# Two rings of weight buffers and sixteen activation buffers, spread over the address modulo 512

## The chip, the cores and the metric

The kernel is one program on one core of a Trainium2 chip. A core has a matrix engine (PE), a vector engine (DVE), a scalar engine (ACT), a general engine (POOL) and a queue engine (SP) that issues most DMAs here. Each engine works through its own list of instructions in order, and engines wait for each other by semaphores. SBUF is the on-chip memory of 128 partitions, PSUM the memory that PE writes its products to. The metric is the time of one execution on the device, in microseconds (us).

## The reference, cut to what matters

Two transformer blocks over 1024 tokens of width 1024, all in float32: the first has two layers (a window attention mixer and a linear recurrence mixer, each with attention to a memory, and an MLP of width 4096), the second has one layer of stick-breaking and sliding-window attention. Nearly all of the arithmetic is in products with weights:

```python
x = x + jnp.concatenate([mixed, mo], axis=-1) @ w_out[l]
x = x + squared_relu_mlp(rms_norm(x, mlp_norm[l]), w_up[l], w_down[l])
def squared_relu_mlp(h, w_up, w_down):
    return jnp.square(jax.nn.relu(h @ w_up)) @ w_down
```

## The kernel before, in words

Activations lie transposed: 128 features on the partitions, 1024 tokens along them, in two halves of 512. A float32 operand is split into two numbers of the matrix engine's type, `hi` and `lo` (`split`: ACT casts to `hi`, DVE subtracts to get `lo`), and a product is three matmuls, hi·hi, lo·hi and hi·lo (`mm3`, L121, L124, L125). Each is a weight load of 128x128 and a matmul of up to 512 columns.

`weight` fetches 128x1024 raw weights by a DMA on SP's queue into a tile `wr`, and splits them into tiles `wh` and `wl`. These two names are rings of four buffers each in the pool `wp`. The activations of the matmuls lie in eight tiles `hh0` to `hh7` and eight `hl0` to `hl7` in the pool `hp` (`h_tiles`; named `uh`, `ul`, `oph`, `opl` where other stages use the same buffers), and in stages that need more in further tiles `xh`, `xl` of the pool `hx`.

The first layer's stages are memory keys, attention, the output projection (`down_groups`), the MLP's up phase and its down phase; the second layer's and the second block's follow in the same manner. The up phase computes 16 units of weights, each by seven half-size products (Strassen's scheme, `up_phase`), out of operands `B11`, `B21`, `T1` to `T4` and `B22` that `first_ops` and `other_ops` make from the normalised activations with DVE, ACT and POOL. `early_products` does what needs `B11` and `B21` alone for the first five units while the others are made. Of one unit, the weights come as two raw tiles; DVE forms sums in `v` (L749 to L751) and in place in the raw tiles, then the pair `yh`, `yl` (for `A11` and `S3`), the pair `xh`, `xl` (for `A22` and `A12`), `vh`, `vl` (for `S1`, `S2`) and `qh`, `ql` (for `S4`) are split. Of the first five units, `A22` is the first half of the second raw tile, which no sum changes before. The y and x pairs come from the same rings `wh` and `wl`.

The order of the instructions on each engine is made when the program is built: a scheduler takes the instructions by priority and by its own model of time, and gives a tile a buffer of its tag when one is free. So a different set of tags can give a different order, though the source's order is the same.

Of the kernel before, what the change touches and what calls it, by code (L numbers as in the profile page):

```python
# [11 lines left out]
F32 = mybir.dt.float32  # L12
F32R = mybir.dt.float32r
# [8 lines left out]
P = 128  # L22
D = 1024
S = 1024
KC = D // P
# [21 lines left out]
def net_kernel(ctx: ExitStack, tc: tile.TileContext, xT, memT, vecs, pos, sinks, invf, mask0, alibi,  # L47
# [5 lines left out]
    wp = ctx.enter_context(tc.tile_pool(name="wp", bufs=1))  # L53
    dp = ctx.enter_context(tc.tile_pool(name="dp", bufs=1, space=DRAM))
    hp = ctx.enter_context(tc.tile_pool(name="hp", bufs=1, side="right"))
# [26 lines left out]
    def nm(base):  # L82
        n_name[0] += 1
        return f"{base}_{n_name[0]}"
# [14 lines left out]
    def split(hi, lo, src, hi_eng=None, lo_eng=dve):  # L99
        if hi_eng is dve:  # L100
            dve.tensor_copy(hi, src)
        else:
            act.copy(hi, src)  # L103
        lo_eng.tensor_tensor(out=lo, in0=src, in1=hi.bitcast(F32), op=ALU.subtract)  # L104
# [5 lines left out]
    def weight(src, n=1024, hi_eng=None, lo_eng=dve):  # L110
        raw = wp.tile([P, 1024], F32, tag="wr", name=nm("wr"), bufs=4)
        nc.sync.dma_start(raw[:, :n], src)
        hi = wp.tile([P, 1024], F32R, tag="wh", name=nm("wh"), bufs=4)
        lo = wp.tile([P, 1024], F32R, tag="wl", name=nm("wl"), bufs=4)
        split(hi[:, :n], lo[:, :n], raw[:, :n], hi_eng, lo_eng)
        return hi, lo

# [86 lines left out]
    def spread(r, n, tmp, psp):  # L204
        dg = tmp.tile([P, 512], F32, tag="sq", name=nm("dg"))
        for j in range(n // P):
            dve.tensor_scalar(out=dg[:, j * P:j * P + P], in0=ident, scalar1=r[:, j:j + 1], scalar2=None, op0=ALU.mult)
        pr = psp.tile([P, 512], F32, tag="po", name=nm("psr"))
        pe.matmul(pr[:, :n], ones, dg[:, :n], start=True, stop=True)
        return pr  # L210

    def norm_r(sums, tmp, psp, rtile, first=False, rtile2=None, keep=None):
# [17 lines left out]
            dve.tensor_copy(keep, r)  # L230
        act.copy(rtile, spread(r, n, tmp, psp)[:, :n])

    def h_tiles():
        hh = [hp.tile([P, S], F32R, tag=f"hh{c}", name=nm("hh")) for c in range(KC)]
        hl = [hp.tile([P, S], F32R, tag=f"hl{c}", name=nm("hl")) for c in range(KC)]
        return hh, hl
# [37 lines left out]
    def down_groups(x, order, load_u, pieces, up, psp, sums, after_half, cuts=(hs(0), hs(1)), halves=False):  # L274
        for gi, gs_ in enumerate(order):
# [4 lines left out]
            def fetch(q, gs_=gs_):  # L280
                ws[q] = [weight(pieces[g * 4 + q]) for g in gs_]
# [160 lines left out]
    hh, hl = h_tiles()  # L442
    with tc.tile_pool(name="s0", bufs=1) as tp, \
# [19 lines left out]
        for l in range(2):  # L463
            mkh = tp.tile([P, 4, ML], F32R, tag="mkh", name=nm("mkh"))
            mkl = tp.tile([P, 4, ML], F32R, tag="mkl", name=nm("mkl"))
            for h in range(4):
                wh, wl = weight(w_memk[l * 4 + h]) if l + h else w00
# [11 lines left out]
            for q in range(4):  # L479
                wh, wl = weight(w_memv[l * 4 + q])  # L480
# [225 lines left out]
    def prod(ps, w, op, start=True):  # L706
        hi, lo, o = w
        mm3(ps, [(hi[:, o + k * P:o + k * P + P], lo[:, o + k * P:o + k * P + P], op[0][k], op[1][k])
                 for k in range(4)], start=start, skip=True)

    def square_out(l, cc, src, f, th):
        act.activation(cc, src, AF.Relu)
        act.activation(cc, cc, AF.Square)
        nc.sync.dma_start(u_d[l][:, f, hs(th)], cc)

    def raw_half(src, parts):
        raw = wp.tile([P, 1024], F32, tag="wr", name=nm("wr"), bufs=4)
        for i, o in enumerate(parts):
            n = 1024 // len(parts)
            nc.sync.dma_start(raw[:, i * n:i * n + n], src[:, o:o + n])  # L720
        return raw

    def early_products(l, ops, tk):
        banks = {}
        for i in range(EARLY + 1):
            if i < EARLY:
                raw = raw_half(w_up[l * 16 + i], (0, 1536))
                hi = wp.tile([P, 1024], F32R, tag="wh", name=nm("wh"), bufs=4)
                lo = wp.tile([P, 1024], F32R, tag="wl", name=nm("wl"), bufs=4)
                split(hi, lo, raw)  # L730
                ps = psp.tile([P, HT], F32, "S", nm("psu"))
                prod(ps, (hi, lo, 0), ops["B11"])
                e1 = tk.tile([P, HT], F32, tag="ru", name=nm("e1"))
                act.copy(e1, ps)
                nc.sync.dma_start(e_d[l][:, i, :], e1)
                banks[i] = (ps, hi, lo)
            if i:
                ps, hi, lo = banks[i - 1]
                prod(ps, (hi, lo, 512), ops["B21"], start=False)
                cc = tk.tile([P, HT], F32, tag="ru", name=nm("cc"))  # L740
                square_out(l, cc, ps, 2 * i - 2, 0)

    def up_phase(l, ops, up):
        def weights(i, part):
            r1 = raw_half(w_up[l * 16 + i], (0,))
            r2 = raw_half(w_up[l * 16 + i], (1024,))
            a11, a21, a22, a12 = r1[:, :512], r1[:, 512:], r2[:, :512], r2[:, 512:]
            v = up.tile([P, 1024], F32, tag="v", name=nm("v"), bufs=1)
            dve.tensor_tensor(out=v[:, :512], in0=a21, in1=a22, op=ALU.add)  # L749
            dve.tensor_tensor(out=a21, in0=a11, in1=a21, op=ALU.subtract)  # L750
            dve.tensor_tensor(out=v[:, 512:], in0=v[:, :512], in1=a11, op=ALU.subtract)  # L751

            def pair():
                return (wp.tile([P, 1024], F32R, tag="wh", name=nm("wh"), bufs=4),
                        wp.tile([P, 1024], F32R, tag="wl", name=nm("wl"), bufs=4))

            (yh, yl), (xh, xl) = pair(), pair()
            y0, x1 = (512, 512) if part else (0, 1024)
            split(yh[:, y0:], yl[:, y0:], r1[:, y0:])
            split(xh[:, :x1], xl[:, :x1], r2[:, :x1])  # L760
            vh = up.tile([P, 1024], F32R, tag="vh", name=nm("vh"), bufs=2)
            vl = up.tile([P, 1024], F32R, tag="vl", name=nm("vl"), bufs=2)
            split(vh, vl, v)
            dve.tensor_tensor(out=a12, in0=a12, in1=v[:, 512:], op=ALU.subtract)
            qh = up.tile([P, 512], F32R, tag="qh", name=nm("qh"), bufs=2)
            ql = up.tile([P, 512], F32R, tag="ql", name=nm("ql"), bufs=2)
            split(qh, ql, a12)
            return {"A11": (yh, yl, 0), "S3": (yh, yl, 512), "A22": (xh, xl, 0), "A12": (xh, xl, 512),
                    "S1": (vh, vl, 0), "S2": (vh, vl, 512), "S4": (qh, ql, 0)}

        def small(tag, bufs):
            return up.tile([P, HT], F32, tag=tag, name=nm(tag), bufs=bufs)

        tail = None
        for i in range(16):
            part = i < EARLY
            w = weights(i, part)
            a = psp.tile([P, HT], F32, "mm", nm("psu"))
            e1 = small("e", 4)
            if part:  # L780
                nc.sync.dma_start(e1, e_d[l][:, i, :])
            else:
                prod(a, w["A11"], ops["B11"])
                act.copy(e1, a)
                b = psp.tile([P, HT], F32, "tr", nm("psu"))
                prod(b, w["A12"], ops["B21"])
                cc = small("cc", 4)
                dve.tensor_tensor(out=cc, in0=e1, in1=b, op=ALU.add)
                square_out(l, cc, cc, 2 * i, 0)
            if tail:  # L790
                tail()
            c = psp.tile([P, HT], F32, "S", nm("psu"))
            prod(c, w["S1"], ops["T1"])

            def add_to(a, e1, part=part):
                t = small("e", 4)
                if part:
                    dve.tensor_tensor(out=t, in0=e1, in1=a, op=ALU.add)
                else:
                    act.copy(t, a)  # L800
                return t

            prod(a, w["S2"], ops["T2"], start=part)
            u1 = add_to(a, e1)
            d = psp.tile([P, HT], F32, "tr", nm("psu"))
            prod(d, w["A22"], ops["T4"])
            prod(a, w["S3"], ops["T3"], start=False)
            u2 = add_to(a, e1)
            cc = small("cc", 4)
            dve.tensor_tensor(out=cc, in0=u2, in1=c, op=ALU.add)  # L810
            square_out(l, cc, cc, 2 * i + 1, 1)
            cc = small("cc", 4)
            dve.tensor_tensor(out=cc, in0=u2, in1=d, op=ALU.subtract)
            square_out(l, cc, cc, 2 * i + 1, 0)

            def tail(i=i, w=w, c=c, u1=u1):
                prod(c, w["S4"], ops["B22"], start=False)
                cc = small("cc", 4)
                dve.tensor_tensor(out=cc, in0=u1, in1=c, op=ALU.add)
                square_out(l, cc, cc, 2 * i, 1)  # L820
        tail()
# [34 lines left out]
    for l in range(2):  # L856
# [169 lines left out]
        with ExitStack() as ph:  # L1026
# [81 lines left out]
            hh, hl = nh[-1]  # L1108
# [349 lines left out]
```

## Time and profile before

| | us |
|---|---|
| three runs | 3061.18, 3063.29, 3067.44 |
| median | 3063.29 |
| the profiled execution | 3062.59 |
| its span, from the first to the last instruction | 3060.8 |

In the profile "PE" is matmuls and "PEld" weight loads, which overlap them. A matmul's duration runs to its modelled end, so consecutive matmuls overlap in the records, and what counts is the distance from start to start. "Idle before" is the time in which an engine did nothing before an instruction, with the instruction that ended it. "PEclk" is the granted clock of TensorE as a share of its upper level of 2.4 GHz; 0.50 is the lower level of 1.2 GHz.

### The profile page before, as it was taken

What the parts mean: (1) busy time and instruction counts of PE and PEld (TensorE: products, weight loads), DVE (VectorE), ACT (ScalarE), POOL (GpSimd) and SP (SyncE); (2) the same over time, 40 slices, a digit from 0 to 9 for tenths busy, and PEclk for the clock granted to TensorE, in tenths of its full rate; (3) what the DMA queues carried; (4) which work ended last, traced back from release to release, by engine and by line L of the source; (5) the groups of instructions that cost most, each with busy time, mean ns of one, the idle gap of its engine ahead of it and who ended that gap; (6) DMA issues with size and microseconds to landing.
All of it is one profiled execution on the core that took longest, in us unless ns stands there. A gap on an engine that the chain in (4) does not pass through costs nothing. (4 is left out here: it accounts for less than half of the span.)

```text
span 3060.8 us, 38811 instructions
## 1 busy us (share of the span) xinstructions
PE 2936.4 (96%) x14624; PEld 2395.3 (78%) x14624; DVE 1793.7 (59%) x3053; ACT 1308.9 (43%) x2408; POOL 395.1 (13%) x428
## 2 busy tenths in 40 slices
PE   8999999989999999998889979999999999999998
PEld 7988778768888888776767858888888777777777
DVE  7666754674457443678874575445343565666555
ACT  6566541444552121356772344554121244444542
POOL 3222100300000000333320210000000211111112
PEclk9999999989999999999999989999999999999999
DMA  7111244343357322221246234237232121111152
GB/s 263 42 49 63 95 169 175 119 148 110 104 175 258 131 97 90 69 66 66 88 159 235 101 107 139 103 125 237 76 104 76 55 76 42 35 42 56 64 178 77
DMA packets 136204, 341.55 MB, mean 112 GB/s; under 512 B 14928, under 2 KB 29520, under 8 KB 136016
## 3 DMA queue, kind: packets, MB, share of 16 engines
q1 hardware_dynamic: 131840, 331.93, 31.7%
q10 hardware_dynamic: 4176, 7.13, 0.7%
q8 instruction: 115, 1.88, 0.3%
q14 instruction: 73, 0.60, 0.1%
HBM read 245.16 MB, written 93.85 MB: 111 GB/s over the span
## 5 line engine op out<-in xcount | busy, mean ns | idle before, releaser
L124 PE MATMUL psd<-ul,wh 128*128 128x512 f32 (+1 forms) x1568 | 606.9, 387 | 1.2 <-DMA ul<-mixl 1.2
L121 PE MATMUL psd<-uh,wh 128*128 128x512 f32 (+1 forms) x1568 | 606.5, 387 | 0.9 <-DVE x L315 0.8
L125 PE MATMUL psd<-uh,wl 128*128 128x512 f32 (+1 forms) x1568 | 606.0, 387 | 0.0
L103 ACT CAST wh<-wr 128x1024 fp32r<-128x1024 f32 (+2 forms) x236 | 234.6, 998 | 729.5 <-PE psd L124 497.0
L104 DVE TENSOR_TENSOR wl<-wr,wh 128x1024 fp32r<-128x1024 f32 (+2 forms) x260 | 311.1, 1199 | 220.9 <-ACT wh L103 219.7
L315 DVE TENSOR_TENSOR x<-x,psd 128x512 f32<-128x512 f32 x288 | 196.5, 685 | 377.4 <-PE psd L125 371.3
L121 PEld LDWEIGHTS psd<-uh,wh 128*128 128x128 f32 x1568 | 294.7, 188 | 61.9 <-issue 2.0
L124 PEld LDWEIGHTS psd<-ul,wh 128*128 128x128 f32 x1568 | 294.7, 188 | 61.3 <-issue 2.1
L125 PEld LDWEIGHTS psd<-uh,wl 128*128 128x128 f32 x1568 | 294.8, 188 | 60.1 <-issue 1.9
L121 PE MATMUL psu<-oph,wh 128*128 128x512 f32 x512 | 200.7, 394 | 41.2 <-ACT wh L103 41.2
L153 POOL TENSOR_TENSOR acc<-acc,sq 128x512 f32<-128x512 f32 (+1 forms) x70 | 94.6, 1352 | 1006.7 <-ACT sq L149 995.6
L124 PE MATMUL psu<-opl,wh 128*128 128x512 f32 x512 | 199.9, 391 | 0.0
L125 PE MATMUL psu<-oph,wl 128*128 128x512 f32 x512 | 199.0, 391 | 0.0
L124 PE MATMUL pj<-hl,wh 128*128 128x512 f32 x416 | 165.1, 401 | 9.1 <-DVE hl L104 9.1
L121 PE MATMUL pj<-hh,wh 128*128 128x512 f32 x416 | 169.3, 411 | 4.3 <-DVE qkl L104 2.2
L125 PE MATMUL pj<-hh,wl 128*128 128x512 f32 x416 | 164.9, 400 | 0.0
L121 PEld LDWEIGHTS psu<-oph,wh 128*128 128x128 f32 x512 | 96.8, 189 | 62.4 <-ACT wh L103 42.1
L124 PEld LDWEIGHTS psu<-opl,wh 128*128 128x128 f32 x512 | 96.7, 189 | 20.4 <-issue 0.5
L125 PEld LDWEIGHTS psu<-oph,wl 128*128 128x128 f32 x512 | 96.6, 189 | 20.2
L121 PE MATMUL psx<-hh,wh 128*128 128x512 f32 x256 | 98.5, 396 | 6.9 <-ACT gl L896 6.9
L121 PE MATMUL psu<-oph,vh 128*128 128x512 f32 x256 | 100.8, 394 | 0.0
L124 PE MATMUL psu<-opl,vh 128*128 128x512 f32 x256 | 100.6, 393 | 0.0
(335 smaller groups left out, 5916.8 us busy)
## 6 DMA issues: line engine op xcount, KB each, us to landing
wr<-in_w_up SPq DMA_DIRECT2D x64, 512.0 KB, 3.9
ud<-cc SPq DMA_DIRECT2D x128, 256.0 KB, 2.2
ur<-ud SPq DMA_DIRECT2D x64, 512.0 KB, 3.6
wr<-in_w_down SPq DMA_DIRECT2D x64, 512.0 KB, 4.0
wr<-in_w_out SPq DMA_DIRECT2D x32, 512.0 KB, 3.6
wr<-in_w_in SPq DMA_DIRECT2D x26, 512.0 KB, 3.5
wra<-in_w_ada SPq DMA_DIRECT2D x24, 512.0 KB, 4.4
uh<-mixh SPq DMA_DIRECT2D x20, 512.0 KB, 8.1
```

The lines of the kernel that those rows point to most:

```text
L103: act.copy(hi, src)
L104: lo_eng.tensor_tensor(out=lo, in0=src, in1=hi.bitcast(F32), op=ALU.subtract)
L121: ins = pe.matmul(out, lh, rh, start=start and i == 0, stop=False, skip_group_check=skip)
L124: pe.matmul(out, lh, rl, start=False, stop=False, skip_group_check=skip)
L125: ins = pe.matmul(out, ll, rh, start=False, stop=stop and i == n - 1, skip_group_check=skip)
L153: pool.tensor_tensor(out=self.acc[:, :n], in0=self.acc[:, :n], in1=sq[:, :n], op=ALU.add)
L315: dve.tensor_tensor(out=xs, in0=xs, in1=ps, op=ALU.add)
```

## The change

The rings `wh` and `wl` become four tags of one buffer each, taken in turn (`ring`), and behind each of these eight buffers lies an unused tile of 16 float32 (64 bytes a partition). Behind each of the sixteen activation buffers lies an unused tile of 8 float32 (32 bytes), set when `h_tiles` is called first. No instruction is added or taken away: the lists of the five engines have the same lengths, and only the order differs.

```diff
-        hi = wp.tile([P, 1024], F32R, tag="wh", name=nm("wh"), bufs=4)
-        lo = wp.tile([P, 1024], F32R, tag="wl", name=nm("wl"), bufs=4)
+        hi = ring("wh")
+        lo = ring("wl")
...
+    pads, used, pads_done = [], {}, []
+
+    def pad(pool_, width):
+        pads.append(pool_.tile([P, width], F32, tag=f"pad{len(pads)}", name=f"pad{len(pads)}"))
+
+    def ring(name):
+        i = used.setdefault(name, 0)
+        used[name] = i + 1
+        t = wp.tile([P, 1024], F32R, tag=f"{name}{i % 4}", name=nm(name))
+        if i < 4:
+            pad(wp, 16)
+        return t
+
     def h_tiles():
+        if not pads_done:
+            pads_done.append(True)
+            hh, hl = [], []
+            for out, t in ((hh, "hh"), (hl, "hl")):
+                for c in range(KC):
+                    out.append(hp.tile([P, S], F32R, tag=f"{t}{c}", name=nm(t)))
+                    pad(hp, 8)
+            return hh, hl
```

`early_products` and the y and x pairs of `up_phase` call `ring` in the same way. The byte addresses within a partition, modulo 512, in the two built programs:

| buffers | before | now |
|---|---|---|
| `wh`, four | 480, each | 480, 96, 224, 352 |
| `wl`, four | 480, each | 32, 160, 288, 416 |
| `hh`, eight | 480, each | 480, 0, 32, 64, 96, 128, 160, 192 |
| `hl`, eight | 480, each | 224, 256, 288, 320, 352, 384, 416, 448 |
| tiles of `hx`, of `x`, of `vh`, `vl`, `qh`, `ql` | 480, each | 480, each |

Of the 11,968 matmuls with split operands, the moving and the stationary operand stood 0 bytes apart modulo 512 in 11,776 before; the other 192, of the memory attention, stood 128 (96) and 384 (96) apart. Now 2,026 stand 0 apart, and each of the other multiples of 32 has 430 to 1,144.

The order differs in the up phase of both layers and in a few places behind them. The first place is where the up phase of the first layer begins. On PE, before: `psu_1329` is the last early product, `wh_1338` the weights of `A22` of unit 0, `oph_1295` and `opl_1297` the first two blocks of `T4`, `vh_1340` the weights of `S1` and `S2`.

```order
L125 MATMUL psu_1329_6501<-oph_1255_6071,wl_1328_6498 128x512
L121 MATMUL psu_1348_6610<-oph_1295_6282,wh_1338_6565 128x512
L124 MATMUL psu_1348_6610<-opl_1297_6284,wh_1338_6565 128x512
L121 MATMUL psu_1346_6583<-oph_1279_6266,vh_1340_6571 128x512
L124 MATMUL psu_1346_6583<-opl_1281_6268,vh_1340_6571 128x512
L121 MATMUL psu_1344_6580<-oph_1287_6274,vh_1340_6571 128x512
L124 MATMUL psu_1344_6580<-opl_1289_6276,vh_1340_6571 128x512
```

On PE now, at the same place; `wh_1357` are the weights of `A22` of unit 1.

```order
L125 MATMUL psu_1329_6525<-oph_1255_6095,wl_1328_6522 128x512
L121 MATMUL psu_1348_6634<-oph_1295_6306,wh_1338_6589 128x512
L121 MATMUL psu_1368_6743<-oph_1295_6306,wh_1357_6681 128x512
L124 MATMUL psu_1348_6634<-opl_1297_6308,wh_1338_6589 128x512
L125 MATMUL psu_1348_6634<-oph_1295_6306,wl_1339_6590 128x512
L121 MATMUL psu_1348_6634<-oph_1295_6306,wh_1338_6589 128x512
L124 MATMUL psu_1368_6743<-opl_1297_6308,wh_1357_6681 128x512
```

All 24 matmuls of the two products with `T4` now stand ahead of the first one with `vh_1340`; two stood there before. The same holds at the start of the second layer's up phase.

On DVE, before, behind the last of the operands: the sums of unit 0 (`v_1335`, and `wr` in place) and the low parts of its weights.

```order
L749 TENSOR_TENSOR v_1335_6559<-wr_1333_6555,wr_1334_6557 128x512
L750 TENSOR_TENSOR wr_1333_6555<-wr_1333_6555 128x512
L751 TENSOR_TENSOR v_1335_6559<-v_1335_6559,wr_1333_6555 128x512
L764 TENSOR_TENSOR wr_1334_6557<-wr_1334_6557,v_1335_6559 128x512
L104 TENSOR_TENSOR wl_1337_6564<-wr_1333_6555,wh_1336_6563 128x512
L104 TENSOR_TENSOR wl_1339_6566<-wr_1334_6557,wh_1338_6565 128x512
L104 TENSOR_TENSOR vl_1341_6572<-v_1335_6559,vh_1340_6571 128x1024
```

On DVE now, some 26 instructions earlier, among the operands:

```order
L104 TENSOR_TENSOR opl_1286_6297<-x_1135_5338,oph_1284_6295 128x512
L104 TENSOR_TENSOR wl_1339_6590<-wr_1334_6581,wh_1338_6589 128x512
L717 TENSOR_TENSOR x_1132_5335<-x_1132_5335 128x512
...
L724 TENSOR_TENSOR x_862_4129<-t2_1299_6317,x_862_4129 128x512
L104 TENSOR_TENSOR opl_1289_6300<-t2_1299_6317,oph_1287_6298 128x512
L104 TENSOR_TENSOR wl_1358_6682<-wr_1353_6673,wh_1357_6681 128x512
```

Two low parts, `wl_1339` and `wl_1358`, have moved ahead of most of the operands, and so have their casts `wh_1338` and `wh_1357` on ACT. The sums of unit 0 still stand behind all operands.

## Rows read from the trace of the kernel before

**Rows 1.** The page: the span, PE's busy time, and PE and its granted clock in 40 slices of the span.

```profile
span 3060.8 us, 38811 instructions
PE 2936.4 (96%) x14624; PEld 2395.3 (78%) x14624; DVE 1793.7 (59%) x3053; ACT 1308.9 (43%) x2408; POOL 395.1 (13%) x428
PE   8999999989999999998889979999999999999998
PEclk9999999989999999999999989999999999999999
```

**Rows 2.** Who PE waited for in the whole span: us in total, times, longest.

```profile
PE psu L121 <- ACT wh L103: 41.2, 2, 21.6
...
PE pj L124 <- DVE hl L104: 9.1, 2, 7.2
...
PE ms L121 <- ACT mp L380: 7.2, 2, 6.8
...
PE psr L209 <- DVE dg L207: 3.8, 2, 3.5
PE pj L121 <- DVE qkl L104: 2.2, 2, 1.9
PE pj L121 <- ACT hh L103: 2.2, 1, 2.2
```

**Rows 3.** Busy time of each engine in stretches around the start of the up phase, in both layers, with the count of instructions: start and end, length, PE, PEld, DVE, ACT, POOL, then the granted clock, DMA share and GB/s.

```profile
606.00:626.00 20.00, 0.44 (x2) 0.01 (x1) 17.99 (x26) 8.58 (x16) 10.03 (x4) 0.58 0.28 92
626.00:629.70 3.70, 3.67 (x8) 2.65 (x9) 3.68 (x6) 1.45 (x2) 0.00 (x0) 0.50 0.40 138
629.70:640.00 10.30, 10.30 (x47) 8.51 (x46) 10.15 (x15) 4.21 (x6) 0.00 (x0) 1.00 0.59 187
640.00:850.00 210.00, 210.00 (x928) 173.98 (x927) 110.82 (x148) 102.73 (x159) 0.00 (x0) 1.00 0.35 119
...
1781.20:1802.90 21.70, 0.09 (x1) 0.00 (x0) 19.69 (x29) 9.42 (x18) 10.97 (x4) 0.55 0.10 34
```

**Rows 4.** PE in order of time at the start of both up phases: start, us, engine, line, operation, tiles. In the first layer, the last early product's last matmul, then the first, second, third, tenth and 25th matmul behind the wait; in the second layer the first.

```profile
606.05 0.39 PE L125 MATMUL psu<-oph,wl 128*128 128x512 f32 x1
626.03 0.79 PE L121 MATMUL psu<-oph,wh 128*128 128x512 f32 x1 [19.60 <-ACT wh L103]
626.63 0.63 PE L124 MATMUL psu<-opl,wh 128*128 128x512 f32 x1
627.05 0.72 PE L121 MATMUL psu<-oph,vh 128*128 128x512 f32 x1
...
629.98 0.39 PE L125 MATMUL psu<-oph,wl 128*128 128x512 f32 x1
...
633.40 0.39 PE L124 MATMUL psu<-opl,vh 128*128 128x512 f32 x1
```

```profile
1802.92 0.79 PE L121 MATMUL psu<-oph,wh 128*128 128x512 f32 x1 [21.63 <-ACT wh L103]
```

**Rows 5.** DVE in order of time in the first of these stretches.

```profile
609.71 0.68 DVE L104 TENSOR_TENSOR opl<-t,oph 128x512 fp32r<-128x512 f32 x1
612.20 1.92 DVE L104 TENSOR_TENSOR opl<-x,oph 128x512 fp32r<-128x512 f32 x2 [1.80 <-ACT oph L103]
...
621.00 2.48 DVE L104 TENSOR_TENSOR opl<-x,oph 128x512 fp32r<-128x512 f32 x4
623.41 0.68 DVE L749 TENSOR_TENSOR v<-wr,wr 128x512 f32<-128x512 f32 x1
624.12 0.69 DVE L750 TENSOR_TENSOR wr<-wr 128x512 f32<-128x512 f32 x1
624.73 0.69 DVE L751 TENSOR_TENSOR v<-v,wr 128x512 f32<-128x512 f32 x1
```

**Rows 6.** ACT in order of time in the same stretch.

```profile
611.55 0.62 ACT L103 CAST oph<-x 128x512 fp32r<-128x512 f32 x1 [3.97 <-POOL x L701]
...
624.84 1.14 ACT L103 CAST wh<-wr 128x512 fp32r<-128x512 f32 x2 [3.72 <-DVE wr L750]
625.89 1.04 ACT L103 CAST vh<-v 128x1024 fp32r<-128x1024 f32 x1
```

**Rows 7.** POOL's subtraction that makes `T4`: all eight of the span (shortest, median and longest in ns), and its place in order of time.

```profile
L701 POOL TENSOR_TENSOR x<-t,x x8: 1264/1645/6459, 605.1 to 1794.0; 128x512 f32<-128x512 f32 x8
```

```profile
605.06 7.69 POOL L701 TENSOR_TENSOR x<-t,x 128x512 f32<-128x512 f32 x2 [22.87 <-DVE t L699]
```

**Rows 8.** PE in order of time: matmuls of 256 columns back to back, first with operands 384 bytes apart modulo 512, then 128, then 0; of each the first and the last of seven.

```profile
343.24 0.29 PE L124 MATMUL ms<-mkl,mqh 128*128 128x256 f32 x1
...
343.96 0.29 PE L125 MATMUL ms<-mkh,mql 128*128 128x256 f32 x1
```

```profile
1577.97 0.28 PE L124 MATMUL ms<-mkl,mqh 128*128 128x256 f32 x1
...
1578.69 0.28 PE L124 MATMUL ms<-mkl,mqh 128*128 128x256 f32 x1
```

```profile
3019.13 0.28 PE L124 MATMUL psd<-ul,wh 128*128 128x256 f32 x1
...
3019.85 0.28 PE L124 MATMUL psd<-ul,wh 128*128 128x256 f32 x1
```

**Rows 9.** The weight loads of the down products, as a group over the span: busy us, mean ns of one.

```profile
L124 PEld LDWEIGHTS psd<-ul,wh 128*128 128x128 f32 x1568 | 294.7, 188 | 61.3 <-issue 2.1 <-DMA ul<-mixl 1.6
```

More of the change, by code (lines that the diff above doesn't have):

```diff
@@ L727, in early_products @@
                 raw = raw_half(w_up[l * 16 + i], (0, 1536))
-                hi = wp.tile([P, 1024], F32R, tag="wh", name=nm("wh"), bufs=4)
-                lo = wp.tile([P, 1024], F32R, tag="wl", name=nm("wl"), bufs=4)
+                hi = ring("wh")
+                lo = ring("wl")
                 split(hi, lo, raw)
@@ L753, in pair @@
             def pair():
-                return (wp.tile([P, 1024], F32R, tag="wh", name=nm("wh"), bufs=4),
-                        wp.tile([P, 1024], F32R, tag="wl", name=nm("wl"), bufs=4))
+                return (ring("wh"),
+                        ring("wl"))
             (yh, yl), (xh, xl) = pair(), pair()
```

## The prediction

> **What bounds the kernel now.** I read the page first. It shows PE busy for 2936.4 of 3060.8 us, with the clock at its upper level in nearly every slice [rows 1]. So the time is the number of PE's matmuls by their spacing, plus some 124 us in which PE does nothing. A change can win or lose in two ways: in the spacing, or in PE's waits.
>
> Then the views that answer for the spacing. In the steady stretch from 640 to 850 us PE starts 928 matmuls of 512 columns in 210.0 us [rows 3], 226.3 ns each. Three short runs of 256-column matmuls have their operands 384, 128 and 0 bytes apart modulo 512; in each, six intervals take 0.72 us, so 120 ns [rows 8]. By the two widths a column costs (226.3 − 120) / 256 = 0.415 ns, and a matmul has a fixed part of 120 − 256 × 0.415 = 13.7 ns. The reader is to see that the three distances give one number.
>
> Last the list of PE's waits. The largest is 41.2 us in two waits for the cast `wh` on ACT [rows 2]. In order of time they are the starts of the two up phases, 19.60 and 21.63 us [rows 4]. In the first, DVE works 17.99 of 20 us, ACT 8.58 and POOL 10.03 [rows 3]: DVE and POOL make the operands `T1` to `T4`, and only then DVE forms the sums of unit 0, and only behind those does ACT cast the weights that PE wants [rows 5, 6]. PE waits though `T4` (`oph` at 611.55 on ACT, `opl` at 612.20 on DVE and behind) has long been there [rows 5, 6].
>
> **The change part by part.** *Addresses.* No instruction writes a pad, so the pads cost nothing as work. 9,750 of the 11,968 split matmuls leave distance 0. The rows show three distances only, all alike to within the 0.01 us of a row over six intervals, some 2 ns. I take 0 for the other thirteen, since they lie among the three shown, and since one matmul streams 2048 bytes of its row past 512 bytes of weights: the distance between what is being read of the two changes all through a matmul. The bounds follow as rivals: distance 0 itself costs the fixed part (13.7 ns by 9,750 is a gain of 134 us), or some distances clash, by at most a whole weight load of 188 ns [rows 9].
>
> *Rings of one buffer.* A tile must now take the next tag of the ring, not the first one free. The buffer that comes late is that of a y pair, which waits for `S3`, the last of a unit, instead of `A22`'s twelve matmuls earlier: 12 × 0.226 = 2.7 us later, against the 84 matmuls, 19 us, of the unit in between. In the steady stretch DVE works 110.8 and ACT 102.7 of 210 us [rows 3], so these casts have the slack: 0. If it were gone, one such wait a unit, 2.7 us by 32 units, would be 86 us; nothing in the rows comes near it.
>
> *The order at the start of the up phases.* `wh_1338`, `wh_1357` and their low parts stand earlier, so the 24 matmuls of `A22` with `T4` can run within the wait. They need `T4` alone of the operands. First what that costs on DVE: two subtractions of 128x512, which follow each other at 0.62 us (four in 2.48 [rows 5]), 1.2 us, placed before the last operands. Before these DVE has 1.80 us idle, waiting for `oph`, and that waits 3.97 us on ACT for POOL's L701 [rows 5, 6]. Does the idle time hide the 1.2 us? POOL's two subtractions start at 605.06 and the slowest of the eight takes 6.46 us where the shortest takes 1.26 [rows 7]. From 605.06 that is an end at 611.52, which is 1.13 us after DVE went idle (609.71 + 0.68 = 610.39 [rows 5]): the subtraction looks as if it had run only once DVE stood still. I take it that it again ends 1.1 us after DVE stops, so that the 1.2 us shift POOL, ACT's `oph` and the whole chain. The Trainium skill, "SBUF — State Buffer", section "Who interferes with whom", says that a DVE instruction with two SBUF inputs and a GpSimd instruction that reads SBUF contend, and that the second to issue "fully blocks"; the 6.46 against 1.26 us agree. By that rule the 1.2 us are paid; by independent engines they vanish in DVE's 1.80 us, and the lead below is larger by 1.2 us a layer.
>
> With the shift, `v` (L751, ended 624.73 + 0.69 = 625.42 [rows 5]) is there at 626.6. ACT casts `vh` next, in 1.04 us [rows 6], with one `wh` cast fewer ahead of it; the first matmul with `vh` starts near 627.8 instead of 627.05 [rows 4].
>
> Now the gain. In the new order this matmul is the 25th from the start of the wait. Before, the 25th started at 633.40 [rows 4]. So PE is 633.4 − 627.8 = 5.6 us ahead, if its clock is then up. Before, it was not: the first eight matmuls took 626.03 to 629.71, 3.68 us at a granted clock of 0.50 (1.2 GHz), after an idle stretch of 19.6 us [rows 3, 4], where 8 × 0.226 = 1.81 us would do. Now 24 matmuls are strewn over the idle stretch, and whether the clock is up at 627.8 isn't shown by any row. With the same loss of 1.87 us the lead is 3.7 us. I take the middle, 4.65 us. The second layer has the same pieces: its wait is 21.63 us, with 19.69 of 21.70 us of DVE [rows 3, 4]. Two layers: 9.3 us, bounds 7.4 and 11.2.
>
> *What is late next.* Behind the first `vh` matmul PE runs at full spacing and DVE has 10.15 busy of 10.30 us [rows 3]: PE, being ahead, asks for `vl` and the pairs of units 1 and 2 sooner. Two low parts less in that stretch give DVE 1.2 us back there, so I count no new wait, and up to 2 us a layer if I am wrong. Further on, PE waits 9.1, 7.2, 3.8, 2.2 and 2.2 us, 24.5 us in all, for DVE and ACT in other stages [rows 2]. A lead helps in such a place only if the engine that ends the wait also gets its work sooner. Most of these waits stand behind norms, which do start from what PE made; others stand behind DVE's own queue. I take a third as given back, 3.1 us; none and three quarters are the ends. These are choices, not readings. The order also moves in the second layer's memory attention, where the 7.2 us wait is; I count it at 0, with ±2 us.
>
> **The sum.** −9.3 + 3.1 = −6.2 us on the profiled execution of 3062.59 us (span 3060.8) is 3056.4 us. That execution is 0.7 us under the median 3063.29, so 3057 us is the forecast. Its own range: nothing given back of 11.2 us, 3052 us, to three quarters of 9.3 given back, 3061 us.
>
> **The rivals.** *The lead is wholly given back.* For it: the 24.5 us of waits behind, and DVE at 10.15 of 10.30 us just after the start [rows 2, 3]. Against it: in the 210 us of steady stretch PE is full, and DVE half idle, so a lead of 5 us lives through the up phase itself. Time: 3063 us, 3060 to 3066.
>
> *Some distances clash (slower).* One place: the matmul's stream and the next weight load reading at addresses that fall on each other. A distance has (11,968 − 2,026) / 15 = 663 matmuls. If one of the 15 costs 18 ns a matmul, it takes 12 us, which beats the gain of 6 by as much again: from there it decides. At the bound, a whole load of 188 ns, it is 125 us (3182 us), at half of that 62 us (3119 us). For it: before, 11,776 matmuls stood at distance 0, so most distances have never been seen. Against it: 128 and 384 show 120 ns like 0 [rows 8]. The same section of the Trainium skill gives PE one read port for the moving operand and an independent one for weight loads, by which no distance could cost anything.
>
> *Distance 0 was the slow one.* Then the fixed part goes for 9,750 matmuls, 134 us, 2929 us, or a part of it. For it: nothing but that the fixed part's cause isn't shown. Against it: the matmuls at 384 and 128 would have to be quicker than those at 0, and are not [rows 8].
>
> **How the numbers follow.** A measurement of this kernel tells from no change about 0.2%, 6.1 us. The forecast has a chance of 0.64; since its middle lies on that bound, 0.34 of it is faster and 0.30 the same. The lead given back has 0.20, all of it the same. A clash, with any other loss of this size, has 0.12, slower. Distance 0 as the culprit has 0.04, faster. That is 0.38, 0.50 and 0.12. The range 3048 to 3068 us takes in the forecast and the lead given back with the ±2 us of the small terms in both layers; it leaves out the culprit and most of the clash, some 0.15.
>
> **What would show it.** In the profile of the changed kernel PE's two waits for `wh` must be gone or split, with matmuls of `psu` on `T4` from about 613 us, and the first with `vh` near 627.8 us; the spacing in the steady stretch must stay at 226 to 227 ns; POOL's slow subtraction must end about 1.2 us later; and what is given back must stand as longer waits for DVE in the stages behind. A spacing off by 1 ns over the 12,000 matmuls, or no lead at 640 us, would make the forecast wrong.

## The result, and the profile after

The changed kernel takes 3096.33 us (median of four runs, 3094.92 to 3100.42) where before takes 3063.38: a ratio of 1.0108, with a 95% interval of 1.0091 to 1.0126. It is 33 us slower. The forecast was 3057 us, the range ended at 3068, and "slower" had a chance of 0.12.

First the page of the changed kernel: span, PE, and PE with its granted clock in 40 slices, to be read beside [rows 1].

```profile
span 3093.1 us, 38763 instructions
PE 2981.6 (96%) x14624; PEld 2392.2 (77%) x14624; DVE 1795.9 (58%) x3053; ACT 1311.1 (42%) x2408; POOL 397.0 (13%) x428
PE   8999999999999999998889989999999989999998
PEclk9999999999999999999999989999999999999999
```

PE does as many matmuls as before, at no lower a granted clock (0.987 in the mean of the span, 0.981 before), and is busy for 45 us more. So the loss is not in waits. Then what PE waited for (us in total, times, longest), beside [rows 2]:

```profile
PE psu L121 <- ACT oph L103: 16.9, 4, 8.8
...
PE pj L124 <- DVE hl L104: 7.6, 3, 6.9
PE psu L124 <- DVE opl L104: 5.6, 2, 2.8
...
PE pj L121 <- DVE qkl L104: 3.8, 2, 3.5
...
PE psu L121 <- ACT vh L103: 1.5, 2, 1.2
```

The 41.2 us for `wh` are gone; 16.9, 5.6 and 1.5 us of waits for operands and for `vh` stand in their place. So PE waits less, as forecast, and the kernel is slower all the same. The stretches of [rows 3] show where (start and end, length, then PE, PEld, DVE, ACT and POOL busy with their counts, granted clock, DMA share, GB/s); the first three are bounded at the last early product, the first matmul with `vh`, and 640 us:

```profile
609.60:626.00 16.40, 6.48 (x16) 4.06 (x16) 14.46 (x21) 7.90 (x14) 10.52 (x4) 0.75 0.32 101
626.00:630.60 4.60, 4.45 (x10) 2.99 (x10) 4.53 (x8) 1.64 (x3) 0.00 (x0) 0.50 0.01 4
630.60:640.00 9.40, 9.32 (x39) 7.44 (x40) 8.97 (x14) 3.35 (x6) 0.00 (x0) 0.96 0.52 174
640.00:850.00 210.00, 210.00 (x908) 170.17 (x906) 114.47 (x153) 105.38 (x160) 0.00 (x0) 1.00 0.36 123
```

The last line is the finding: PE is full at the upper clock, DVE has 95 us free, and yet it starts 908 matmuls in 210 us and not 928, one every 231.3 ns and not every 226.3. A busy engine can be a slower engine; only the count beside the busy time tells.

PE in order of time at the start of the first up phase, beside [rows 4]:

```profile
609.36 0.40 PE L125 MATMUL psu<-oph,wl 128*128 128x512 f32 x1
616.28 1.22 PE L121 MATMUL psu<-oph,wh 128*128 128x512 f32 x2 [6.53 <-ACT oph L103]
...
622.29 0.73 PE L121 MATMUL psu<-oph,wh 128*128 128x512 f32 x2 [0.60 <-ACT oph L103]
625.81 0.80 PE L124 MATMUL psu<-opl,wh 128*128 128x512 f32 x1 [2.79 <-DVE opl L104]
...
630.68 0.79 PE L121 MATMUL psu<-oph,vh 128*128 128x512 f32 x1 [0.23 <-ACT vh L103]
631.28 0.44 PE L124 MATMUL psu<-opl,vh 128*128 128x512 f32 x1
631.56 0.40 PE L121 MATMUL psu<-oph,vh 128*128 128x512 f32 x1
631.79 0.40 PE L124 MATMUL psu<-opl,vh 128*128 128x512 f32 x1
```

The 24 matmuls of `A22` run where PE had waited, from 616.28 us on, and the first one with `vh`, the 25th, starts 21.3 us after the last early product (forecast: 627.8 − 606.05, 21.8). Before, the 25th started 27.3 us after it (606.05 to 633.40 [rows 4]). The lead is there, 6.0 us.

### The profile page after: what moved, and what is told of

Same layout as the page of the kernel before. It is cut to its first block, busy times and chain, and to the rows that moved or that the text cites. A ratio compares the mean times of both kernels' runs of the same rounds, so it can differ in the third digit from the quotient of the medians.

```text
span 3093.1 us, 38763 instructions
## 1 busy us (share of the span) xinstructions
PE 2981.6 (96%) x14624; PEld 2392.2 (77%) x14624; DVE 1795.9 (58%) x3053; ACT 1311.1 (42%) x2408; POOL 397.0 (13%) x428
## 4 chain that ended last, share of the span: by engine, by line
PE 81%; DVE 9%; ACT 5%; issue 4%; POOL 1%; DMA 0%; DVEq 0%; SPq 0%; ACTq 0%; POOLq 0%
PE psd L125 11%; PE psd L121 11%; PE psd L124 11%; PE psu L121 6%; PE psu L125 6%; PE psu L124 6%; PE pj L121 3%; PE pj L124 3%; PE pj L125 3%; PE po L640 2%; PE z L1209 1%; PE po L1238 1%; PE psp L121 1%; PE psp L124 1%; PE psp L125 1%
## 5 line engine op out<-in xcount | busy, mean ns | idle before, releaser
L121 PE MATMUL psd<-uh,wh 128*128 128x512 f32 (+1 forms) x1568 | 614.1, 392 | 1.0 <-DVE x L336 0.8
L125 PE MATMUL psd<-uh,wl 128*128 128x512 f32 (+1 forms) x1568 | 613.2, 392 | 0.0
L124 PE MATMUL psd<-ul,wh 128*128 128x512 f32 (+1 forms) x1568 | 612.4, 391 | 0.0
L124 PEld LDWEIGHTS psd<-ul,wh 128*128 128x128 f32 x1568 | 295.4, 188 | 68.5 <-issue 2.4
L121 PEld LDWEIGHTS psd<-uh,wh 128*128 128x128 f32 x1568 | 294.9, 188 | 68.1 <-issue 2.0
L125 PEld LDWEIGHTS psd<-uh,wl 128*128 128x128 f32 x1568 | 294.7, 188 | 67.4 <-issue 2.0
L121 PE MATMUL psu<-oph,wh 128*128 128x512 f32 x512 | 203.4, 402 | 16.9 <-ACT oph L103 16.9
L124 PE MATMUL psu<-opl,wh 128*128 128x512 f32 x512 | 204.6, 400 | 5.6 <-DVE opl L104 5.6
L125 PE MATMUL psu<-oph,wl 128*128 128x512 f32 x512 | 201.3, 400 | 0.0
L121 PE MATMUL pj<-hh,wh 128*128 128x512 f32 x416 | 171.1, 415 | 6.9 <-DVE qkl L104 3.8
L124 PE MATMUL pj<-hl,wh 128*128 128x512 f32 x416 | 167.1, 405 | 7.6 <-DVE hl L104 7.6
L125 PE MATMUL pj<-hh,wl 128*128 128x512 f32 x416 | 167.3, 405 | 0.0
L121 PEld LDWEIGHTS psu<-oph,wh 128*128 128x128 f32 x512 | 97.2, 191 | 41.2 <-ACT oph L103 18.7
L124 PEld LDWEIGHTS psu<-opl,wh 128*128 128x128 f32 x512 | 98.1, 192 | 31.0 <-DVE opl L104 7.7
L125 PEld LDWEIGHTS psu<-oph,wl 128*128 128x128 f32 x512 | 97.9, 191 | 22.9
L121 PE MATMUL psx<-hh,wh 128*128 128x512 f32 x256 | 100.1, 402 | 9.0 <-ACT gl L917 9.0
L121 PE MATMUL psu<-oph,vh 128*128 128x512 f32 x256 | 101.8, 398 | 1.5 <-ACT vh L103 1.5
L121 PEld LDWEIGHTS pj<-hh,wh 128*128 128x128 f32 x416 | 79.4, 191 | 30.3 <-DVE qkl L104 4.4
```

The lines of the kernel that those rows point to most:

```text
L121: ins = pe.matmul(out, lh, rh, start=start and i == 0, stop=False, skip_group_check=skip)
L124: pe.matmul(out, lh, rl, start=False, stop=False, skip_group_check=skip)
L125: ins = pe.matmul(out, ll, rh, start=False, stop=stop and i == n - 1, skip_group_check=skip)
```

## The experiments

Theory A, formed from this profile: a matmul costs more when the address of its moving operand and that of the weights differ modulo some power of two. Theory B: the new order costs, by work of other engines beside the matmuls. Theory C: it is not the distance that costs but that it changes from matmul to matmul.

**The order alone.** The rings of one buffer, no pad (the edit of the changed kernel).

```diff
-        if i < 4:
-            pad(wp, 16)
...
-                    pad(hp, 8)
```

> The rings of one buffer without any pad: the order of the instructions is that of the changed kernel, all addresses are 480 modulo 512 as before. Theory A (the distance between the moving operand and the weights modulo 512 sets the spacing of the matmuls, and any other than 0 costs some 5 ns): spacing back at 226 to 227 ns, and the lead at the start of the up phases kept, 3057 us (3052 to 3061). Theory B (the new order itself costs, by other work of DVE, ACT and DMA beside the matmuls): spacing stays at some 231 ns, 3096 us.

Measured: 3062.06 us, ratio 0.9988 (0.9979 to 0.9997). The order and the rings cost nothing; B falls. The time is above the 3052 to 3061 that I gave, since the lead isn't kept to the end (below). In the steady stretch the spacing is that of before: 925 matmuls and a gap of 0.47 us.

```profile
640.00:850.00 210.00, 209.53 (x925) 173.24 (x924) 117.80 (x157) 105.62 (x161) 0.00 (x0) 1.00 0.37 123
```

This kernel has the same list of matmuls as the changed one, so the two traces can be laid beside each other, matmul by matmul, from start to start. Worked out from the two traces:

| intervals | count | rings alone, us | changed kernel, us | difference |
|---|---|---|---|---|
| 512 columns, up to 300 ns in both | 9,486 | 2145.2 | 2189.1 | +43.9 |
| 512 columns, longer (waits, lower clock) | 546 | 270.7 | 258.3 | −12.4 |
| 384 columns, up to 300 ns | 995 | 184.2 | 185.0 | +0.8 |
| 256 columns, up to 300 ns | 831 | 107.8 | 107.6 | −0.2 |
| all others | 2,765 | 336.4 | 335.9 | −0.4 |

The sum is 31.6 us, against 31.4 between the spans (3093.1 and 3061.7). So the pads cost 43.9 us in the 512-column matmuls, 4.6 ns each, and next to nothing in the others. 12.4 us come back, and hardly by shorter waits: 11.3 of them stand in matmuls that ran at the lower clock in one of the two traces alone, 91 in that of the rings and 29 in that of the changed kernel (granted clock 0.982 and 0.987 in the mean). The other runs that pay for a distance get back 2.7 to 9.2 us in the same class, those that don't at most 1.7. Why the clock fell less often, no run shows.

**The activation pads alone.** Rings and order of before (the edit of the kernel before).

```diff
+            for out, t in ((hh, "hh"), (hl, "hl")):
+                for c in range(KC):
+                    out.append(hp.tile([P, S], F32R, tag=f"{t}{c}", name=nm(t)))
+                    pad(hp, 8)
```

> Only the 32-byte pads behind the sixteen activation buffers; rings and order are those of before. 7,192 of the 11,968 split matmuls leave distance 0. Theory A: 7,192 by 5 ns is 36 us, 3099 us (3085 to 3115), and the products with activations in these buffers show 230 to 234 ns, those with the other tiles 226 to 227. Theory B: 3063 us and 226 to 227 ns everywhere.

Measured: 3093.72 us, ratio 1.0095 (1.0081 to 1.0108). The pads of the activations are enough for nearly the whole loss.

**The weight pads alone**, with the rings (the edit of the changed kernel):

```diff
-                    pad(hp, 8)
```

> The change without the pads of the activation buffers: rings of one buffer and the order of the change, weights 64 bytes further apart each, activations all at 480. Distances are multiples of 64. Theory A (every matmul whose own or next weights are not a multiple of 256 away costs some 6 ns, whatever else): 6,784 split matmuls have their own weights off, so up to 41 us of spacing, three quarters of it as time: 3093 us (3085 to 3100). Rival (the pads of weights and those of activations add up to the 33 us of the change, of which the activations alone cost 30): 3066 us.

Measured: 3090.81 us, ratio 1.0084 (1.0065 to 1.0103), as theory A had it. The weights' pads alone cost 27 us, the activations' alone 30, both together 33: they don't add up. A matmul that already stands off pays no second time, as the run with `wl` moved shows below.

**One distance for all.** The sixteen activation buffers moved together, by 32, 128, 224 or 256 bytes; order of before. For 32 (the two pads add up to 512 bytes, so that nothing else moves modulo 512):

```diff
+            pad(hp, 8)
+            for out, t in ((hh, "hh"), (hl, "hl")):
+                for c in range(KC):
+                    out.append(hp.tile([P, S], F32R, tag=f"{t}{c}", name=nm(t)))
+            pad(hp, 120)
```

> Order of before; all sixteen activation buffers moved by the same 32 bytes: 7,872 split matmuls stand 32 (or 480) apart, one and the same distance from matmul to matmul. Theory A: in the changed kernel those 32 apart took 231.5 ns, 4.8 ns more than at 0 before; 7,872 by 4.8 is 38 us, 3101 us. Theory C (only a distance that changes from matmul to matmul costs): 3063 us.

> Order of before; all sixteen activation buffers moved by the same 256 bytes, so that 7,872 split matmuls stand 256 apart and the rest as before. Theory A with a period of 512: in the changed kernel the matmuls 256 apart took 229.9 ns, 3 ns more than at 0 before; 7,872 by 3 is 24 us, 3087 us. Theory A with a period of 256 (rivals of 256 and 0 are then alike): 3063 us. Theory C (not the distance costs, but that it changes from one matmul to the next): 3063 us as well.

> Order of before; all sixteen activation buffers moved by 128 bytes, the farthest there is with a period of 256. Theory A with any distance alike: as with 32 bytes, 3098 us and some 233 ns. Theory A with a cost that grows with the distance: four times that of 32 bytes, some 255 ns and 3200 us. Rival (only distances that are no multiple of 128 cost, which would agree with the 256-column matmuls 128 apart of before): 3063 us.

> Order of before; all sixteen activation buffers moved by 224 bytes, which with a period of 256 is 32 bytes the other way. Theory A with any distance alike: some 233 ns, 3098 us. If only the side matters on which the weights lie (the stream following or leading the load): 227 ns, 3063 us.

Measured: 32 bytes 3098.65 us, ratio 1.0109 (1.0095 to 1.0123); 128 bytes 3097.98 us, 1.0110 (1.0090 to 1.0130); 224 bytes 3099.73 us, 1.0116 (1.0096 to 1.0136); 256 bytes 3063.40 us, 0.9997 (0.9987 to 1.0006). The steady stretch, first with 32 bytes, then with 256:

```profile
640.00:850.00 210.00, 210.00 (x910) 170.35 (x909) 110.91 (x149) 99.38 (x155) 0.00 (x0) 1.00 0.35 117
```

```profile
640.00:850.00 210.00, 210.00 (x928) 173.90 (x927) 112.40 (x150) 101.41 (x158) 0.00 (x0) 1.00 0.34 117
```

One constant distance costs as much as the mixture: theory C falls. A distance of 256 costs nothing, and 32, 128 and 224 cost the same: a period of 256 bytes, no growth with the distance, no better side. My rivals "four times as much at 128" and "only what is no multiple of 128" fall too.

Inside the trace of the 32-byte run both kinds stand side by side, as some operands lie in other pools: 6,188 intervals of 512-column matmuls with operands 32 apart are 233.4 ns long in the mean, 2,857 with operands 0 apart 227.9 (both with neighbours that don't wait).

**Distance or address?** In the 32-byte run the moving operands also came to lie at 0 modulo 512. So everything was moved by 32 bytes, weights too:

```diff
+        if not lead:
+            lead.append(wp.tile([P, 8], F32, tag="lead", name="lead"))
         raw = wp.tile([P, 1024], F32, tag="wr", name=nm("wr"), bufs=4)
...
+            pad(hp, 120)
```

> Order of before; the weight buffers, the activation buffers and every tile beside them are all moved by 32 bytes, to 0 modulo 512, so that every distance between operands stays what it was. In the run with activations moved by 32 bytes the moving operands stood at 0 too, so the address itself could have cost, not the distance. Theory A (distance, with a period of 256): spacing 226 to 227 ns, 3063 us (3060 to 3067). Rival (the address 0 of the moving operand costs): spacing 233 ns, 3098 us.

Measured: 3062.97 us, ratio 0.9995 (0.9985 to 1.0005), 928 matmuls in the steady stretch:

```profile
640.00:850.00 210.00, 210.00 (x928) 173.93 (x928) 112.01 (x151) 100.73 (x157) 0.00 (x0) 1.00 0.35 119
```

It is the distance, not the address.

**Which distance: to its own weights, or to the next ones?**

```diff
         hi = wp.tile([P, 1024], F32R, tag="wh", name=nm("wh"), bufs=4)
+        if not lead:
+            lead.append(wp.tile([P, 32], F32, tag="lead", name="lead"))
         lo = wp.tile([P, 1024], F32R, tag="wl", name=nm("wl"), bufs=4)
+        if len(lead) < 2:
+            lead.append(wp.tile([P, 96], F32, tag="lead2", name="lead2"))
```

> Order of before; only the low weights wl (of the ring) moved by 128 bytes. Of each product of three matmuls hi.wh (L121), lo.wh (L124), hi.wl (L125) the last one streams against weights 128 bytes away (own distance), and the middle one streams while the weights 128 bytes away are loaded for its successor (next distance). If the own distance costs: L125 some 233 ns, L121 and L124 227. If the next distance costs: L124 some 233 ns, the others 227. Either way one matmul in three: 3,488 by 6 ns is 21 us, of which the experiments before gave some three quarters as time: 3079 us (3070 to 3087). If both must be off 0: no change, 3063 us.

Measured: 3090.53 us, ratio 1.0086 (1.0071 to 1.0101), outside the 3070 to 3087 that I gave: not one matmul in three pays, but two. The groups of the down products by line and of the up products with `vh`, whose weights were not moved (busy us, mean ns of one | idle before); L127, L130 and L131 are L121, L124 and L125 of before. First the same groups before, then in this run:

```profile
L121 PE MATMUL psd<-uh,wh 128*128 128x512 f32 x1504 | 588.4, 391 | 0.9 <-DVE x L315 0.8
L124 PE MATMUL psd<-ul,wh 128*128 128x512 f32 x1504 | 588.4, 391 | 1.2 <-DMA ul<-mixl 1.2
L125 PE MATMUL psd<-uh,wl 128*128 128x512 f32 x1504 | 587.7, 391 | 0.0
...
L121 PE MATMUL psu<-oph,vh 128*128 128x512 f32 x256 | 100.8, 394 | 0.0
L124 PE MATMUL psu<-opl,vh 128*128 128x512 f32 x256 | 100.6, 393 | 0.0
```

```profile
L131 PE MATMUL psd<-uh,wl 128*128 128x512 f32 x1504 | 598.6, 398 | 0.0
L130 PE MATMUL psd<-ul,wh 128*128 128x512 f32 x1504 | 597.7, 397 | 1.3 <-DMA ul<-mixl 1.3
L127 PE MATMUL psd<-uh,wh 128*128 128x512 f32 x1504 | 588.2, 391 | 0.8 <-DVE x L321 0.8
...
L127 PE MATMUL psu<-oph,vh 128*128 128x512 f32 x256 | 100.7, 393 | 0.0
L130 PE MATMUL psu<-opl,vh 128*128 128x512 f32 x256 | 100.5, 393 | 0.0
```

`uh·wh`, with its own and the next weights 0 apart, has 391 ns; `ul·wh`, whose own weights stand at 0 but whose successor's don't, 397; `uh·wl`, whose own weights are 128 away, 398. From start to start that is 227.2, 232.4 and 233.9 ns (3,842, 2,538 and 2,601 intervals). Either place is enough here, and both together cost no more: 234.0 ns (61).

Two things stay open. In both kinds that pay here, the own and the next weights also stand 128 bytes from each other, so this run can't tell a distance to the stream from a distance between the two weights; in the 32-byte run the weights don't differ among themselves, and the matmuls pay all the same. And at other widths the next weights alone may cost less: in the changed kernel, where they stand off by 64 or 192 bytes, 841 intervals are 229.6 ns long, no more than those with neither off there, and 232.5 to 232.8 where the own weights are off.

**A mixture without cost.** The changed kernel with wider pads:

```diff
-            pad(wp, 16)
+            pad(wp, 64)
...
-                    pad(hp, 8)
+                    if c % 2 == 0:
+                        pad(hp, 64)
```

> The changed kernel with other widths of its pads alone: 256 bytes behind each weight buffer, 256 bytes behind every second activation buffer, none behind the others. The order is that of the changed kernel, word for word; the distance from matmul to matmul goes between 0 (6,912 split matmuls) and 256 (4,864). Theory A with a period of 256 (only distances that are no multiple of 256 cost): spacing 226 to 227 ns, and the time of the rings without pads, 3062 us (3057 to 3065). Rival (a distance that changes from one matmul to the next costs as well): above 3070 us, and spacing of 229 ns or more.

Measured: 3062.70 us, ratio 0.9995 (0.9986 to 1.0004), and the spacing of before. The distance flips between 0 and 256 all the time (2,540 matmuls stand 256 from their own weights and 0 from the next, and last 227.3 ns from start to start), and nothing is lost. So the 33 us of the change hang on the width of its pads alone.

```profile
640.00:850.00 210.00, 209.59 (x925) 173.20 (x924) 116.83 (x156) 107.01 (x163) 0.00 (x0) 1.00 0.36 122
```

**An attempt at keeping the lead.** The rings alone gave only 1.9 us, and their trace shows why (below). With one buffer of each ring in a tag of its own and three in another, the order differs from before in the up phases alone. The edit of the changed kernel, whose pads are taken out as well:

```diff
-        t = wp.tile([P, 1024], F32R, tag=f"{name}{i % 4}", name=nm(name))
+        t = wp.tile([P, 1024], F32R, tag=name + ("a" if i % 4 == 0 else "b"), name=nm(name), bufs=1 if i % 4 == 0 else 3)
```

> No pads; each ring is one tag of one buffer and one tag of three instead of four of one. The order then differs from before in the two up phases alone, where 14 matmuls stand ahead of the first one with vh (before 2, rings of one buffer 26, with two of other products among them); the memory attention of the second layer and the start of the second block keep the order of before. Theory (the lead of the rings of one buffer was lost to the new order of the memory attention and of the second block): some 12 by 0.226 is 2.7 us a layer less 0.6 us for one subtraction, kept to the end: 3060 us (3057 to 3061). Rival (the second block takes any lead back, whatever its order): a lead of 4 us at 2400 us in the trace, none behind 2500 us, and 3064 us.

Measured: 3064.63 us, ratio 1.0003 (0.9993 to 1.0012). It doesn't tell my theory from its rival, since no lead came about. PE at the start of the first up phase:

```profile
607.81 0.39 PE L125 MATMUL psu<-oph,wl 128*128 128x512 f32 x1
628.23 0.79 PE L121 MATMUL psu<-oph,wh 128*128 128x512 f32 x1 [20.04 <-ACT wh L103]
```

I had counted how many matmuls stand ahead of the first one with `vh`, and not looked at what the first of them waits for: at their head stands one whose `wh` is still cast behind the sums. A queue works through its list in order, so it is its head that counts. No version of these beats before by more than the rings alone, at 0.9988.

## Why the prediction was wrong, point by point

*Addresses: the step that failed.* "I take 0 for the other thirteen, since they lie among the three shown, and since one matmul streams 2048 bytes of its row past 512 bytes of weights: the distance between what is being read of the two changes all through a matmul." Both reasons were bad. The three distances shown came from 256-column matmuls [rows 8], and matmuls of 256 columns, as the table above shows, pay nothing; the forecast was for 10,032 matmuls of 512 columns. Of these, 7,872 now had their own weights at no multiple of 256 bytes, others the next ones; in the mean over the 9,486 of the table's first line, a matmul took 4.6 ns more, 43.9 us where I had put 0. And the argument on the stream was no row at all.

The clash rival named the right pair, PE's stream and the weights, and had the wrong size: it put a large price (18 to 188 ns) on one distance in fifteen. Measured is a small price on the distances that are no multiple of 256 bytes: 5 to 7 ns where one distance stood for all, and in the mixture of the changed kernel from 0.8 ns (64 bytes from both weights, 244 intervals) to 7.2 (96 bytes, 233), each against the same matmuls of the rings alone. The Trainium skill, "SBUF — State Buffer", section "Who interferes with whom", gives PE one read port for the moving operand and an independent one for weight loads; I had used it against this rival. That the two reads don't disturb each other does not hold in these runs: 227 and 233 ns at one clock, with the same order, and the distance between the operands alone moved. The measurement decides; where on the way from SBUF the time goes, it doesn't show.

*The order at the start of the up phases: right.* The lead was worked out as 4.65 us a layer (3.7 to 5.6). The rings alone show it without the pads. Counted along PE's list, a matmul there starts later than the same one of before by 2.6 us ahead of the first up phase and earlier by 2.3 behind its start: 4.9 us gained. In the second layer it goes from 1.1 later to 4.2 earlier: 5.4 us.

*POOL's subtraction: right.* In the changed kernel, POOL's subtractions (x8: shortest, median and longest in ns, then the first two in order of time), and DVE beside them:

```profile
L722 POOL TENSOR_TENSOR x<-t,x x8: 1266/1656/7062, 608.5 to 1809.9; 128x512 f32<-128x512 f32 x8
```

```profile
608.51 8.29 POOL L722 TENSOR_TENSOR x<-t,x 128x512 f32<-128x512 f32 x2 [23.48 <-DVE t L720]
```

```profile
613.77 0.68 DVE L104 TENSOR_TENSOR opl<-t,oph 128x512 fp32r<-128x512 f32 x1
616.25 1.92 DVE L104 TENSOR_TENSOR opl<-x,oph 128x512 fp32r<-128x512 f32 x2 [1.80 <-ACT oph L103]
```

DVE stops at 613.77 + 0.68 = 614.45; POOL ends at 608.51 + 7.06 = 615.57, 1.12 us later, as it was 1.13 before; and DVE is idle for 1.80 us as before, though two subtractions more stand ahead. DVE's work in front of this place is paid in full. That agrees with the rule of the Trainium skill, "SBUF — State Buffer", section "Who interferes with whom", that the later of the two blocks; here POOL stays blocked behind a whole row of DVE's instructions, which runs without a gap from 608.35 to 614.45 us.

*The clock: better than the middle I took.* At 630.68 us the first matmul with `vh` still has a spacing of 0.60 us, the next 0.28, and from then mostly 0.23; 630.60 to 640 us has 0.96. The lower clock was mostly spent on the `A22` matmuls, which had time.

*The lead given back: mis-sized.* I gave back a third, 3.1 us. The rings alone lose 0.8 us of the first lead within the up phase, 3.1 at the second layer's memory attention (1.97 earlier to 1.14 later), and 4.7 at the start of the second block (4.21 earlier to 0.53 later): 8.6 of 10.2 us. In that last place PE waits as follows in the run of the rings alone (start, us, what; in brackets idle before and what ended it):

```profile
2444.23 1.22 PE L124 MATMUL pj<-hl,wh 128*128 128x512 f32 x2 [8.03 <-DVE hl L104]
...
2480.42 0.50 PE L121 MATMUL pj<-hh,wh 128*128 128x512 f32 x1 [3.56 <-DVE qkl L104]
...
2488.16 0.51 PE L121 MATMUL pj<-hh,wh 128*128 128x512 f32 x1 [1.76 <-ACT hh L103]
```

The longest waits for `hl` and `qkl` there were 7.2 and 1.9 us before [rows 2]. So the rival "the lead is wholly given back" holds nearly for the order, and would have been the result without the pads. Whether the new order of the memory attention and of the second block took it, or whether any order would, the runs don't settle.

One number must be read with care: the 2.6 us by which the rings' profiled run starts late arise in its first 110 us, and two runs with the order of before start late too, by 3.0 (moved by 256) and 4.7 us (all moved by 32). They are the scatter of single runs, no part of the change.

## What to carry to other kernels

For 512-column matmuls like these, each with a weight load of its own, keep the moving operand and the weights, its own and the next ones, a multiple of 256 bytes apart in their partition; 32 bytes of padding in the wrong place cost 1% here, and pads of 256 bytes nothing. When a profile shows PE full, count its matmuls in a fixed stretch before asking who waits. And a row bounds a cost only for its own shape: 256 columns said nothing of 512.

## What the runs showed of the hardware, and I had not expected

The spacing of back-to-back 512-column matmuls of this kernel, at a granted clock of 1.00, is 227.1 ns (9,016 intervals of the kernel before) when the moving operand, its own weights and the next weights are congruent modulo 256 bytes, and 232 to 234 ns in the runs where one distance of 32, 128 or 224 stood for all, or 128 for one of the two. At 384 columns it is 174 ns at 0 and 174 ns at 224 apart (32-byte run: 589 intervals at 224; before: 726 at 0), and at 256 columns 119 and 117 ns (0 and 32 apart, 230 and 182 intervals). So nearly all of the price is that of the widest matmul. At 384 columns it isn't nothing everywhere: with `wl` moved, 250 matmuls that came to stand 128 apart took 3.0 ns more than the same ones before (186.2 and 183.2 in the mean, those at the lower clock included). In the changed kernel matmuls whose own and next weights are both congruent take 229.6 ns (1,005 intervals), so a neighbour's distance seems to reach over a little. Why 256 bytes, and why nearly only at 512 columns, no run here shows.
